# Value chunks in pairs and the output projection in passes of 512 columns

## The chip, the core and the metric

The kernel runs on one core of a Trainium2 chip. The metric is the device time of one execution in microseconds (us). Engines are named as the profile names them: PE (TensorE matmuls), PEld (TensorE weight loads), DVE (VectorE), ACT (ScalarE), POOL (GpSimd), SP (SyncE, which issues the DMAs here).

## The reference

Two layers of a decoder trunk on 256 tokens of width 1024. Each layer normalises x, projects it with one wide matrix, runs four token mixers (block-sparse, three-branch, stick-breaking and dilated attention, called a to d), gates and widens their outputs, merges them with sigmoid gates, and projects the sum back onto x:

```python
def _hybrid_layer(x, norm_w, w_in, cmp_pos, cmp_w1, cmp_w2, w_up, w_out):
    h = _rmsnorm(x, norm_w)
    proj = jnp.einsum('bsd,dc->bsc', h, w_in)          # q, k, v, gates of a..d, merge gates
    ...
    u = jnp.einsum('bsiw,iwd->bsid', widened, w_up)
    y = jnp.sum(merge_g * u, axis=2)
    return x + y @ w_out

def reference(x, ...):
    for layer in range(DEPTH):                          # DEPTH = 2
        x = _hybrid_layer(x, ...)
    return _rmsnorm(x, final_norm_w)
```

The change concerns three products: the values of mixers a and c (columns `av` and `cv` of `w_in`, 256 each) and `y @ w_out` (1024 columns in four blocks of 256, o0 to o3).

## The kernel before

Every product with a weight is made of three products in float32r: the weight is split into a high part (`wh`, an ACT cast) and a low part (`wl`, a DVE subtraction), the activations likewise (`hh` and `hl`), and hi x hi, hi x lo and lo x hi are summed in PSUM. `hh[0]`, `hl[0]` hold the normalised input, `hh[1]`, `hl[1]` hold y, both as 8 slices of the contraction (k = 0 to 7) x 256 tokens.

Weights come as blocks of 128 x 1024 floats ("halves", one DMA each on SP's queue) into 5 `raw` buffers, and from there into 6 buffers each of `wh` and `wl`. `emit_loads`, `run_splits`, `need_splits` and `release` (lines 312 to 376) keep that going; `release` gives a block's buffers back when its last matmul has been emitted.

The program is written out by a planner in Python. `layer_items` (line 36) lists the chunks of a layer: first the pair `('N2', ('av', 'cv'))`, then chunks of queries, keys, gates and values, then 16 pairs of merge (M) and widening (U) chunks, then o0, o1 and the pair o2/o3. `slots_of` (line 1177) turns a chunk into slots, each a generator of matmuls; the main loop (line 1320) runs them and between their steps lets `fill` emit waiting steps of attention and of evacuations. A clock model (`Clock`, `Engine.cost`, line 154) books each instruction, a float32r matmul with 0.000426 us per column, and `pos` holds when each block is due. All engines run their instructions in the order in which they were emitted.

There are two kinds of weight matmul. In T, M and U chunks the weight is stationary and 256 tokens stream. In N chunks (values, o0 to o3) the activations of one 128-token tile are stationary and 256 weight columns stream. The pair av/cv is emitted by `mm_N2` (line 521), which at each step takes the (token tile, chunk, k pair, product) whose operands are ready first and puts the transposes of token tile 1's normalised input (`norm_T`) in between; chunk j accumulates in bank j, both token tiles side by side. `mm_o0` (line 579) does k = 0 to 5 of both token tiles before k = 6, 7, which come last out of the widening stage. o1, o2, o3 use `mm_N`, one slot per token tile and column block.

After a slot of the projection, `out_done` and `post_out` (lines 1123, 1245) add the bank to x (DVE), square it for the norm (ACT) and, in the last layer, multiply with the final norm weight. When a token tile has all four blocks, `norm_a` makes 1/rms and scales the two halves of x; `norm_b` transposes them. For token tile 0 of layer 0 `norm_b` is emitted ahead of the last of the four slots of o2/o3:

```python
if kind == "N2" and name[0] == "o2" and si == 3 and l + 1 < L:
    norm_b(0, pend.pop(0), l + 1)
```

Of the eight PSUM banks three (`pp`) rotate for weight products.

Of the kernel before, what the change touches and what calls it, by code (L numbers as in the profile page):

```python
# [16 lines left out]
L = 2  # L17
# [18 lines left out]
def layer_items():  # L36
# [6 lines left out]
    it += [("N", "o0", 2), ("N", "o1", 2), ("N2", ("o2", "o3"), 4)]  # L43
# [148 lines left out]
def kernel(ctx: ExitStack, tc: tile.TileContext, x_in, w_half, w_kvb, w_up, norm_w, pe_in,  # L192
# [108 lines left out]
    for l, kind, name, n in items:  # L301
        d = {"U": 1.3, "W1": 0.6}.get(kind, 2.6)
        for j in range(n):
            pos.append(p_)
            if not (kind in ("N", "N2", "K") and j % 2 == 0):
                p_ += d if kind not in ("N", "N2", "K") else 2 * d
# [214 lines left out]
    def mm_N2(banks, h0, pend, l):  # L521


        left = {h: 12 for h in range(4)}
        count = [0, 0]
        todo = [(tt, j, kk, p) for tt in range(2) for j in range(2) for kk in range(4) for p in range(3)]
        waits = [(1, j) for j in range(2)]

        def operands(tt, j, kk, p):
            h = h0 + 2 * j + kk // 2  # L530
            if h not in los or (tt, kk // 2) in waits:
                return None
            a = (hh, hh, hl)[p][0][:, 2 * kk:2 * kk + 2, 128 * tt:128 * tt + 128]
            return a, (his, los, his)[p][h]

        n = 0
        while todo:
# [24 lines left out]
            tt, j, kk, p = b  # L562
# [7 lines left out]
            h = 2 * j + kk // 2  # L570
            left[h] -= 1
            if not left[h]:
                release(h0 + h)
            n += 1
            if n % 3 == 0:
                yield
        yield

    def mm_o0(banks, h0):

        for ks in ((0, 1, 2, 3, 4, 5), (6, 7)):
            for tt in range(2):
                for k in ks:
                    hi, lo = (w[h0 + k // 4][:, 256 * (k % 4):256 * (k % 4) + 256] for w in (his, los))
                    a, b = (y[1][:, k, 128 * tt:128 * tt + 128] for y in (hh, hl))
                    o = banks[tt][:, 0:256]
                    mm(o, a, hi, start=(k == 0), stop=False)
                    mm(o, a, lo, start=False, stop=False)
                    mm(o, b, hi, start=False, stop=(k == KT - 1))
                    if k % 2:  # L590
                        yield
# [102 lines left out]
    def post_stack(l, name, bank):  # L694
# [9 lines left out]
        qkv.put(q)  # L704

# [417 lines left out]
    def post_out(l, c, tt, bank):  # L1123
        xs = xt[:, tt, 256 * c:256 * c + 256]
        vec.scalar_tensor_tensor(out=xs, in0=bank[:, 0:256], scalar=0.25, in1=xs, op0=ALU.mult, op1=ALU.add)
        pp.put(bank)
        square(tt, 256 * c, 256 * c + 256, c)
        if l == L - 1:
            if c == 0:
                fin[tt] = [qkv.get(), qkv.get()]  # L1130
            vec.tensor_tensor(out=fin[tt][c // 2][:, 256 * (c % 2):256 * (c % 2) + 256], in0=xs,
                              in1=nws[L][:, 256 * c:256 * c + 256], op=ALU.mult)
# [44 lines left out]
    def slots_of(l, kind, name, h0):  # L1177

        if kind == "N2" and name[0] == "o2":
            for tt in range(2):  # L1180
                for j in range(2):
                    bank = pp.get()
                    yield (lambda: mm_N(bank[:, 0:256], tt, h0 + 2 * j, 256, hh[1], hl[1]),
                           lambda: out_done(l, 2 + j, tt, bank), [h0 + 2 * j, h0 + 2 * j + 1] if tt else [])
        elif kind == "N2":
            banks = [pp.get(), pp.get()]
            yield (lambda: mm_N2(banks, h0, pend.pop(1), l),
# [297 lines left out]
```

## Time and profile before

| | us |
|---|---|
| median of 3 runs (634.63 to 635.20) | 634.83 |
| the profiled execution | 634.86 |
| its span, first to last instruction | 632.9 |
| PE busy | 612.2 (5192 matmuls) |
| DVE busy | 482.1 |
| ACT busy | 369.5 |

The profile is of one execution. Times in its rows are microseconds from the span's start unless marked ns. A matmul's row gives its start and a modelled duration; matmuls are pipelined, so the distance between two starts is what a pass costs when PE is full. `out<-in` names the tile written and the tiles read; "[0.74 <-PE pp]" behind a row says how long the engine was idle before it and on whom it waited.

### The profile page before, as it was taken

What the parts mean: (1) busy time and instruction counts of PE and PEld (TensorE: products, weight loads), DVE (VectorE), ACT (ScalarE), POOL (GpSimd) and SP (SyncE); (2) the same over time, 40 slices, a digit from 0 to 9 for tenths busy, and PEclk for the clock granted to TensorE, in tenths of its full rate; (3) what the DMA queues carried; (4) which work ended last, traced back from release to release, by engine and by line L of the source; (5) the groups of instructions that cost most, each with busy time, mean ns of one, the idle gap of its engine ahead of it and who ended that gap; (6) DMA issues with size and microseconds to landing.
All of it is one profiled execution on the core that took longest, in us unless ns stands there. A gap on an engine that the chain in (4) does not pass through costs nothing.

```text
span 632.9 us, 12881 instructions
## 1 busy us (share of the span) xinstructions
PE 612.2 (97%) x5192; PEld 587.3 (93%) x5192; DVE 482.1 (76%) x850; ACT 369.5 (58%) x657; POOL 46.3 (7%) x59
## 2 busy tenths in 40 slices
PE   7999999999999999999999999999989999999996
PEld 6999999999998999999999899889989989999995
DVE  5887788999976665677688678899999666566673
ACT  5636744655557888445474564543575678864452
POOL 3020100111200000000001101021110000000000
PEclk9999999999999999999999999999999999999998
DMA  8942456644444345677666155645437344466811
GB/s 282 335 147 79 155 192 243 238 162 148 142 161 153 127 140 168 214 246 237 210 211 227 43 192 167 234 168 208 158 100 223 112 166 150 136 205 193 291 62 67
DMA packets 34907, 112.22 MB, mean 177 GB/s; under 512 B 4256, under 2 KB 5280, under 8 KB 34848
## 3 DMA queue, kind: packets, MB, share of 16 engines
q1 hardware_dynamic: 34560, 111.07, 52.2%
q8 instruction: 41, 0.67, 0.4%
q0 software_dynamic: 144, 0.33, 0.3%
q14 instruction: 18, 0.15, 0.1%
q10 hardware_dynamic: 144, 0.00, 0.0%
HBM read 109.61 MB, written 2.10 MB: 177 GB/s over the span
## 4 chain that ended last, share of the span: by engine, by line
PE 64%; DVE 20%; ACT 7%; issue 6%; DMA 2%; POOL 1%; SPq 0%; POOLq 0%; ACTq 0%; DVEq 0%
PE pp L151 55%; DVE wl L151 8%; DVE rope L151 4%; PE psO L151 3%; PE psT L151 3%; ACT p L151 3%; PE psS L151 3%; ACT wh L151 2%; DVE xt L151 2%; DMA raw<-w_half_dram 2%; DVE hl L151 1%; DVE p L151 1%; DVE pd L151 1%; DVE qkv L151 1%; ACT hh L151 1%
## 5 line engine op out<-in xcount | busy, mean ns | idle before, releaser
L151 PE MATMUL pp<-hh,wh 128*128 128x256 f32 x1008 | 288.2, 286 | 2.2 <-DVE xt L151 1.8
L151 PE MATMUL pp<-hh,wl 128*128 128x256 f32 x1008 | 282.1, 280 | 4.5 <-DVE wl L151 4.4
L151 PE MATMUL pp<-hl,wh 128*128 128x256 f32 x1008 | 280.9, 279 | 0.0
L151 DVE TENSOR_TENSOR wl<-raw,wh 128x1024 fp32r<-128x1024 f32 (+2 forms) x198 | 233.1, 1196 | 48.0 <-ACT wh L151 47.2
L151 ACT CAST wh<-raw 128x1024 fp32r<-128x1024 f32 (+2 forms) x198 | 189.2, 979 | 53.7 <-DMA raw<-w_half_dram 24.3
L151 PEld LDWEIGHTS pp<-hh,wh 128*128 128x128 f32 x1008 | 189.4, 188 | 9.0 <-issue 5.5
L151 PEld LDWEIGHTS pp<-hh,wl 128*128 128x128 f32 x1008 | 189.5, 188 | 6.2 <-DVE wl L151 6.1
L151 PEld LDWEIGHTS pp<-hl,wh 128*128 128x128 f32 x1008 | 189.4, 188 | 0.1
L151 PE MATMUL pp<-wh,hh 128*128 128x256 f32 (+1 forms) x320 | 84.9, 285 | 1.0 <-ACT hh L151 1.0
L151 PE MATMUL pp<-wl,hh 128*128 128x256 f32 (+1 forms) x320 | 83.1, 279 | 1.3 <-DVE wl L151 1.2
L151 PE MATMUL pp<-wh,hl 128*128 128x256 f32 (+1 forms) x320 | 83.4, 281 | 0.0
L151 PEld LDWEIGHTS pp<-wh,hh 128*128 128x128 f32 x320 | 58.3, 192 | 2.5 <-ACT hh L151 1.7
L151 PEld LDWEIGHTS pp<-wl,hh 128*128 128x128 f32 x320 | 57.3, 188 | 1.9 <-DVE wl L151 1.9
L151 PEld LDWEIGHTS pp<-wh,hl 128*128 128x128 f32 x320 | 58.0, 191 | 0.0
L151 ACT ACTIVATE p<-p,small 128x128 f32<-128x128 f32 x96 | 40.0, 449 | 27.8 <-DVE small L151 27.1
L151 DVE TENSOR_TENSOR rope<-pp,sinF 32x512 f32<-32x512 f32 x72 | 49.5, 687 | 3.3 <-PE pp L151 1.4
L151 POOL TENSOR_TENSOR xt<-xt,rope 128x512 f32<-128x512 f32 x14 | 28.0, 1998 | 168.8 <-DVE xt L151 93.2
L151 PE MATMUL pp<-widl,wh 128*128 128x256 f32 x128 | 35.9, 281 | 1.1 <-DVE widl L151 1.1
L151 PE MATMUL pp<-widh,wh 128*128 128x256 f32 x128 | 36.0, 282 | 0.0
L151 PE MATMUL pp<-widh,wl 128*128 128x256 f32 x128 | 35.8, 279 | 0.0
L151 ACT ACTIVATE tm<-pp 128x512 f32<-128x512 f32 x32 | 18.9, 591 | 22.1 <-PE pp L151 22.1
L151 ACT COPY ptr<-psT 128x384 f32<-128x384 f32 x47 | 21.4, 478 | 17.6 <-PE psT L151 17.5
(142 smaller groups left out, 666.6 us busy)
## 6 DMA issues: line engine op xcount, KB each, us to landing
raw<-w_half_dram SPq DMA_DIRECT2D x178, 512.0 KB, 4.2
raw<-w_up_dram SPq DMA_DIRECT2D x32, 256.0 KB, 3.2
raw<-w_kvb_dram SPq DMA_DIRECT2D x4, 536.0 KB, 4.5
xt<-x_in_dram SPq DMA_DIRECT2D x4, 256.0 KB, 3.5
xt<-x_in_dram SPq DMA_DIRECT2D x2, 512.0 KB, 7.1
pd<-norm_w_dram SPq DMA_DIRECT2D x2, 512.0 KB, 5.6
x_mem<-xt SPq DMA_DIRECT2D x2, 512.0 KB, 5.4
xt<-x_mem SPq DMA_DIRECT2D x2, 512.0 KB, 6.0
```

The lines of the kernel that those rows point to most:

```text
L151: return f(*a, **k)
```

## The change

The pair av/cv and the two pairs o0/o1 and o2/o3 are done in passes of 512 columns, the widest that one PSUM bank holds. A weight block holds two k slices of all 512 columns of a pair (before: four k slices of 256 columns); the host packs them so (`n2_type`). Each token tile has a bank of its own. o0 and o1 become a pair; its order is k = 0 to 5 of both token tiles, then k = 6, 7 of both. o2/o3 runs token tile 0, then token tile 1; in the last layer token tile 1 is kept in two passes of 256 columns. `post_out` handles n column blocks at once. The values are copied out of PSUM in four pieces of 256 columns, each on the engine (ACT or DVE) that the plan has free first, after the pair's last matmul. The planner's due times and the slot index at which `norm_b` is emitted are adapted (6 of 8 slots instead of 3 of 4).

The diff, cut to its core:

```diff
-    it += [("N", "o0", 2), ("N", "o1", 2), ("N2", ("o2", "o3"), 4)]
+    it += [("N2", ("o0", "o1"), 4), ("N2", ("o2", "o3"), 4)]
...
     def mm_N2(banks, h0, pend, l):
-        left = {h: 12 for h in range(4)}
+        left = [6] * 4
         count = [0, 0]
-        todo = [(tt, j, kk, p) for tt in range(2) for j in range(2) for kk in range(4) for p in range(3)]
+        todo = [(tt, j, p) for tt in range(2) for j in range(4) for p in range(3)]
...
             for i in range(2):
-                k = 2 * kk + i
-                c = count[j]
-                count[j] += 1
-                mm(banks[j][:, 256 * tt:256 * tt + 256], x[0][:, i, :], x[1][:, 256 * (k % 4):256 * (k % 4) + 256],
-                   start=(c == 0), stop=(c == 47))
...
+                c = count[tt]
+                count[tt] += 1
+                mm(banks[tt], x[0][:, i, :], x[1][:, 512 * i:512 * i + 512], start=(c == 0), stop=(c == 23))
...
-            if n % 3 == 0:
+            if n % 2 == 0:
                 yield
...
-    def mm_o0(banks, h0):
...
+    def mm_o(bank, tt, h0, j, c0, c1):
+
+        for i in range(2):
+            k = 2 * j + i
+            hi, lo = (w[h0 + j][:, 512 * i + c0:512 * i + c1] for w in (his, los))
+            a, b = (y[1][:, k, 128 * tt:128 * tt + 128] for y in (hh, hl))
+            o = bank[:, 0:c1 - c0]
+            mm(o, a, hi, start=(k == 0), stop=False)
+            mm(o, a, lo, start=False, stop=False)
+            mm(o, b, hi, start=False, stop=(k == KT - 1))
+            yield
...
+    def post_copy2(l, names, banks):
+
+        for j, name in enumerate(names):
+            T_[l, name] = take(qkv)
+        for tt in range(2):
+            for j, name in enumerate(names):
+                copy_to(T_[l, name][:, 256 * tt:256 * tt + 256], banks[tt][:, 256 * j:256 * j + 256])
+            pp.put(banks[tt])
...
-    def post_out(l, c, tt, bank):
-        xs = xt[:, tt, 256 * c:256 * c + 256]
-        vec.scalar_tensor_tensor(out=xs, in0=bank[:, 0:256], scalar=0.25, in1=xs, op0=ALU.mult, op1=ALU.add)
+    def post_out(l, c, n, tt, bank):
+
+        c0, c1 = 256 * c, 256 * (c + n)
+        xs = xt[:, tt, c0:c1]
+        vec.scalar_tensor_tensor(out=xs, in0=bank[:, 0:c1 - c0], scalar=0.25, in1=xs, op0=ALU.mult, op1=ALU.add)
         pp.put(bank)
-        square(tt, 256 * c, 256 * c + 256, c)
+        square(tt, c0, c1, c)
...
     def slots_of(l, kind, name, h0):
-        if kind == "N2" and name[0] == "o2":
+        if kind == "N2" and name[0] == "o0":
+
+            banks = [pp.get(), pp.get()]
+            for js in ((0, 1, 2), (3,)):
+                for tt in range(2):
+                    for j in js:
+                        yield (lambda: mm_o(banks[tt], tt, h0, j, 0, 512),
+                               (lambda: out_done(l, 0, 2, tt, banks[tt])) if j == 3 else None, [h0 + j] if tt else [], j, tt)
+        elif kind == "N2" and name[0] == "o2":
             for tt in range(2):
-                for j in range(2):
+                last = l == L - 1 and tt
+                for c0, c1 in ((0, 256), (256, 512)) if last else ((0, 512),):
                     bank = pp.get()
...
+                    for j in range(4):
+                        yield (lambda: mm_o(bank, tt, h0, j, c0, c1),
+                               (lambda: out_done(l, 2 + c0 // 256, (c1 - c0) // 256, tt, bank)) if j == 3 else None,
+                               [h0 + j] if tt and c1 == 512 else [], j, tt)
...
-                if kind == "N2" and name[0] == "o2" and si == 3 and l + 1 < L:
+                if kind == "N2" and name[0] == "o2" and si == 6 and l + 1 < L:
                     norm_b(0, pend.pop(0), l + 1)
...
+    def n2_type(w):
+        w = w.reshape(KT, 128, 512).transpose(1, 0, 2)
+        return [w[:, 2 * j:2 * j + 2].reshape(128, -1) for j in range(4)]
```

## Rows read from the trace of the kernel before

**Rows 1.** Page, section 1: busy us, share of the span, instructions.

```profile
PE 612.2 (97%) x5192; PEld 587.3 (93%) x5192; DVE 482.1 (76%) x850; ACT 369.5 (58%) x657; POOL 46.3 (7%) x59
```

**Rows 2.** Stages: stretch, us, busy us by engine (count), PEclk, DMA share, GB/s.

```profile
15.00:24.30 9.30, 9.30 (x84) 9.30 (x83) 7.70 (x9) 6.12 (x7) 0.00 (x0) 1.00 0.96 331
24.30:296.00 271.70, 267.13 (x2286) 256.07 (x2286) 213.17 (x382) 163.53 (x290) 19.62 (x20) 1.00 0.53 177
296.00:330.00 34.00, 33.98 (x296) 33.31 (x295) 23.88 (x33) 17.74 (x33) 1.11 (x2) 1.00 0.65 205
330.00:604.80 274.80, 268.99 (x2298) 257.38 (x2297) 214.53 (x383) 164.03 (x290) 19.48 (x20) 1.00 0.52 175
604.80:626.30 21.50, 21.50 (x192) 21.50 (x191) 13.04 (x23) 7.98 (x20) 0.55 (x1) 1.00 0.11 40
```

**Rows 3.** Timeline of PE, projection of layer 0: start us, us, instruction.

```profile
307.15 0.28 PE L151 MATMUL pp<-wh,hl 128*128 128x256 f32 x1
...
314.97 0.28 PE L151 MATMUL pp<-wh,hl 128*128 128x256 f32 x1
```

**Rows 4.** Timeline of PE, a merge chunk of layer 0.

```profile
177.25 0.28 PE L151 MATMUL pp<-hh,wh 128*128 128x256 f32 x1
...
179.25 0.28 PE L151 MATMUL pp<-hh,wl 128*128 128x256 f32 x1
```

**Rows 5.** Timeline of PE, one score call of branch b in layer 0.

```profile
191.50 0.87 PE L151 MATMUL psS<-hl,hh 128*128 128x256 f32 x4
192.20 0.28 PE L151 MATMUL pp<-hh,wh 128*128 128x256 f32 x1
```

**Rows 6.** Instruction groups by shape: engine, operation, out<-in xcount | busy us, mean ns.

```profile
L151 PE MATMUL psS<-hl,hh 128*128 128x512 f32 x8 | 2.5, 396 | 0.0
L151 DVE SCALAR_TENSOR_TENSOR tm<-tm,pp 128x512 f32<-128x512 f32 x24 | 16.4, 683 | 4.3 <-ACT tm L151 2.4 <-PE pp L151 1.9
L151 DVE SCALAR_TENSOR_TENSOR xt<-pp,xt 128x256 f32<-128x256 f32 x16 | 6.7, 421 | 6.2 <-PE pp L151 6.2
L151 ACT ACTIVATE rope<-xt 128x256 f32<-128x256 f32 x16 | 6.7, 418 | 23.1 <-DVE xt L151 23.1
L151 ACT ACTIVATE rope<-xt 128x512 f32<-128x512 f32 x4 | 2.5, 629 | 2.6 <-DMA xt<-x_in_dram 2.5
```

**Rows 7.** Timeline of PE, bkv chunk of layer 1, next chunk's first

```profile
342.10 0.29 PE L151 MATMUL pp<-wh,hh 128*128 128x268 f32 x1
...
347.92 0.28 PE L151 MATMUL pp<-wh,hl 128*128 128x268 f32 x1
349.12 0.35 PE L151 MATMUL pp<-hh,wh 128*128 128x256 f32 x1 [0.91 <-DVE xt L151]
```

**Rows 8.** Timeline of PE, passes of 32 columns.

```profile
138.31 1.08 PE L151 MATMUL psS<-kct,qkv 128*128 128x32 f32 x8 [0.21 <-DVE kct L151]
```

**Rows 9.** Timeline of PE, the first weight passes of the kernel.

```profile
10.57 0.63 PE L151 MATMUL pp<-wh,hh 128*128 128x256 f32 x2
...
11.21 0.41 PE L151 MATMUL pp<-wh,hl 128*128 128x256 f32 x1
```

**Rows 10.** Timeline of DVE and PE at the layer boundary.

```profile
312.56 0.43 DVE L151 SCALAR_TENSOR_TENSOR xt<-pp,xt 128x256 f32<-128x256 f32 x1 [0.74 <-PE pp L151]
...
314.45 1.42 DVE L151 SCALAR_TENSOR_TENSOR qkv<-xt,rstd,pd 128x512 f32<-128x512 f32 x2 [0.67 <-POOL rstd L151]
...
315.26 1.32 PE L151 MATMUL psT<-iden,qkv 128*128 128x128 f32 x8
...
321.76 1.41 DVE L151 SCALAR_TENSOR_TENSOR qkv<-xt,rstd,pd 128x512 f32<-128x512 f32 x2 [0.66 <-POOL rstd L151]
...
323.47 0.60 PE L151 MATMUL psT<-iden,qkv 128*128 128x128 f32 x4
```

**Rows 11.** Timeline of SP's queue at the end.

```profile
623.62 6.24 SPq L1144 DMA_DIRECT2D out_dram<-qkv  x4
```

**Rows 12.** Timeline of DVE behind the first value pair.

```profile
26.15 3.60 DVE L151 TENSOR_TENSOR wl<-raw,wh 128x1072 fp32r<-128x1072 f32 x3 [1.14 <-ACT wh L151]
```

More of the change, by code (lines that the diff above doesn't have):

```diff
@@ L302 @@
         d = {"U": 1.3, "W1": 0.6}.get(kind, 2.6)
+        if kind == "N2":
+            pos += [p_ + 1.3 * j for j in range(n)]
+            p_ += 4 * d
+            continue
         for j in range(n):
             pos.append(p_)
-            if not (kind in ("N", "N2", "K") and j % 2 == 0):
-                p_ += d if kind not in ("N", "N2", "K") else 2 * d
+            if not (kind in ("N", "K") and j % 2 == 0):
+                p_ += d if kind not in ("N", "K") else 2 * d
     state = dict(at=0, pos=0.0, load=0, hi=0, lo=0)
@@ L704, in post_stack @@
         qkv.put(q)
+    def post_copy2(l, names, banks):
[5 more added lines that the diff above has]
+            pp.put(banks[tt])
+        done.update((l, name) for name in names)
+        return
+        yield
     def post_copy(l, name, bank):
@@ L1243, with out_done @@
     pend = {}
-    def out_done(l, c, tt, bank):
-        post_out(l, c, tt, bank)
-        if c == 3:
+    def out_done(l, c, n, tt, bank):
+        post_out(l, c, n, tt, bank)
+        if c + n == 4:
             if l + 1 < L:
@@ L1294 @@
         weighted(0, 0)
-        square(0, 512, 1024, 1)
+        square(0, 512, 1024, 2)
         norm_rstd(0)
@@ L1298 @@
         square(1, 0, 512, 0)
-        square(1, 512, 1024, 1)
+        square(1, 512, 1024, 2)
         scaled(0, 0, "v")
@@ L1327 @@
             gen = slots_of(l, kind, name, h0)
-            for si, (work, after, freed) in enumerate(gen):
-                if kind == "N2" and name[0] == "o2" and si == 3 and l + 1 < L:
+            for si, (work, after, freed, *part) in enumerate(gen):
+                if kind == "N2" and name[0] == "o2" and si == 6 and l + 1 < L:
                     norm_b(0, pend.pop(0), l + 1)
@@ L1333 @@
                     lo_, hi_ = h0 + si, h0 + si + 1
-                elif kind == "N2" and name[0] == "av":
-                    lo_, hi_ = h0, h0 + 1
                 elif kind == "N2":
-                    lo_, hi_ = h0 + 2 * (si % 2), h0 + 2 * (si % 2) + 2
+                    j, tt = part or (0, 0)
+                    lo_, hi_ = h0 + j, h0 + j + 1
                 else:
@@ L1340 @@
                 state["at"] = lo_
-                first = pos[lo_] + (2.6 if kind in ("N", "K") and si else 0.0)
+                first = pos[lo_] + (2.6 if kind in ("N", "K") and si else 5.2 if kind == "N2" and tt else 0.0)
                 if kind == "W1":
@@ L1349 @@
                     ins = [hl[0]]
-                else:
-                    tt = si // 2 if kind == "N2" else si
-                    ins = [hl[1 if name[0][0] == "o" else 0][:, :, 128 * tt:128 * tt + 128]]
+                elif kind == "N2" and part:
+                    ins = [hl[1][:, 2 * j:2 * j + 2, 128 * tt:128 * tt + 128]]
+                else:
+                    tt = 0 if kind == "N2" else si
+                    ins = [hl[0][:, :, 128 * tt:128 * tt + 128]]
                 run_splits(HORIZON)
@@ L1405, in t_type @@
         return [w[:, :, 128 * j:128 * j + 128].reshape(128, -1) for j in range(w.shape[2] // 128)]
+    def n2_type(w):
+        w = w.reshape(KT, 128, 512).transpose(1, 0, 2)
+        return [w[:, 2 * j:2 * j + 2].reshape(128, -1) for j in range(4)]
     for l in range(L):
         for kind, name, n in layer_items():
-            for nm in (name if kind == "N2" else (name,)):
-                if kind in ("N", "N2") and nm[0] == "o":
-                    c = int(nm[1])
-                    half += n_type(w_out[l][:, 256 * c:256 * c + 256])
-                elif kind in ("N", "N2"):
+            if kind == "N2":
+                if name[0][0] == "o":
+                    c = 256 * int(name[0][1])
+                    half += n2_type(w_out[l][:, c:c + 512])
+                else:
+                    half += n2_type(np.concatenate([w_in[l][:, cols[nm]:cols[nm] + 256] for nm in name], axis=1))
+            for nm in () if kind == "N2" else (name,):
+                if kind == "N":
                     half += n_type(w_in[l][:, cols[nm]:cols[nm] + 256])
```

45 lines of the change are left out of this document (11 added, 34 removed).

## The prediction

> **What bounds the kernel now.** I read the page's first section, then a table of stages, then the PE timeline inside each stage. TensorE (PE) is busy 612.2 of the 632.9 us, and no other engine comes near [rows 1]. The table shows where that is whole: in the three stretches that the change rewrites, the end of the first value pair (15.0 to 24.3), the layer boundary with the output projection and the second value pair (296 to 330) and the last projection (604.8 to 626.3), PE is busy for 9.30 of 9.30, 33.98 of 34.00 and 21.50 of 21.50 us [rows 2]. So there time can come only from what one pass costs, from passes that vanish, or from a new stop. PE's own stops lie in the two long stretches between (267.13 of 271.70 and 268.99 of 274.80 busy) [rows 2], which the diff doesn't touch by name.
>
> A busy engine of pipelined passes is not read by durations (280 ns each, overlapping) but by distances between starts. From 307.15 to 314.97 lie 69 passes of 256 columns: 7.82 / 69 = 0.1133 us each [rows 3]. The same shape runs at a second pace: from 177.25 to 179.25 lie 17, 0.1176 us each [rows 4]. PE's granted clock reads 1.00 in the stages of both [rows 2]. The trace holds long stretches of either pace and changes between them abruptly, so I treat them as two paces, 0.1133 and 0.1178 (the mean over the slow stretches). The three rewritten stretches run at the fast one.
>
> **The change, part by part.** *Passes.* Per layer the value pair has 96 passes of 256 columns, o0 and o1 together 96, o2 and o3 together 96. All become half as many of 512 columns, except the second token tile of o2 and o3 in the last layer, which keeps 48 of 256. That merges 144 pairs in layer 0 and 120 in layer 1, 264 in all; PE goes from 5192 matmuls to 4928. Columns stay the same, so the only question is whether one pass of 512 costs less than two of 256, 2 x 0.1133 = 0.2267.
>
> The trace of before has passes of 512 columns in the same number type: two groups of eight in the scores of branch b [rows 6]. One score call is two passes of 256 and two of 512, and takes 192.20 - 191.50 = 0.70 us; the 256s around run at the slow pace, so a 512 takes (0.70 - 2 x 0.1178) / 2 = 0.232 us [rows 5]. Three other calls that I read so give 0.70 to 0.72. That is 1.97 times the 256 beside it. The cost goes with columns, and little of it is per pass. How to carry this over to stretches at the fast pace is open: scaled by the pace it is 0.232 x 0.1133 / 0.1178 = 0.223, unscaled 0.232. I take the middle, 0.228: 264 x (0.228 - 0.2267) = **+0.3 us**. Ends: below, columns alone at the full level of the clock. The kernel's first passes run at half the pace, three of them from 10.57 to 11.21, 0.2133 each [rows 9], so 512 columns at the full level are 0.2133: 264 x (0.2133 - 0.2267) = -3.5 us. Above, twice the slow pace, 0.2356: +2.4 us.
>
> A rule speaks for a larger gain. The Trainium skill, page "TensorE: Matmul & The Clock Gate", section "Wait — 56ns, not 53.3ns?", gives a warm pass its columns at 2.4 GHz plus a fixed 2.5 ns, 215.7 ns at 512 columns. By it the term would be 264 x (0.2157 - 0.2267) = -2.9 us. The trace's 0.232 for 512 columns [rows 5] and 0.1133 for 256 [rows 3] don't agree with it, so it stays a rival's sentence.
>
> *Layer boundary, token tile 0.* Its last two column blocks were added and squared one after the other; only the second block's add (0.421, DVE) and square (0.418, ACT) stood on the chain to the next layer's normalisation. Now one add of 512 and one square of 512 stand there: 0.683 and 0.629 by the rows of those shapes [rows 6], so +0.26 and +0.21, **+0.47 us**. Does it show? The chain is add at 312.56, scaled halves from 314.45 on DVE, transposes on PE from 315.26 [rows 10]. The pass before the transposes starts at 314.97 [rows 3]; at the pace of 0.1133 the transposes would have come at 315.08, so PE already waits 0.18 us for that chain and nothing hides more. The change puts the transposes after the same share of token tile 1's columns (half), so all of it shows. Bounds 0.3 (one of the two steps partly hidden) and 0.9 (the square queues behind half a cast on ACT).
>
> *Token tile 1.* The same +0.47, hidden: its scaled halves are done at 321.76 + 1.41 = 323.17, the transposes are placed at 323.47 and later [rows 10], and the 48 passes of the next value pair on token tile 0 (48 x 0.1133 = 5.4 us) are there to fill. Uncovered it would be 0.2 us more. 0.
>
> *Copies of the value pair.* Two ACT copies of 512 become four of 256, shared between ACT and DVE by the planner, emitted after the last pass. They wait for the pair's last pass, and behind them on DVE stands a weight subtraction of the next chunk; DVE has 1.14 us of idle time at that place [rows 12], two copies of some 0.35 fit. If that cover goes, the stop of 0.91 us behind DVE [rows 7], where PE waits for a bank that the rotation frees, grows by up to 0.7 in each layer. 0.
>
> *Weight blocks.* Same bytes, same number of loads; a block now holds two of the eight k slices for 512 columns. The first matmuls of a pair need one block instead of two, and the last two y slices are needed after 36 passes of 512 (8 us) instead of 36 of 256 (4 us): looser, but PE doesn't wait there now. Four blocks are held through o0 and o1 instead of two; six buffers leave two for the next pair and blocks come back from the middle on. No load on SP's queue moves past another. 0.
>
> *Start and end.* PE has no idle time in 15 to 24.3 [rows 2], so an earlier operand buys nothing. At the end the last 48 passes and what follows them are as before; token tile 0's output leaves 0.5 later than 623.62, where four issues take 6.24 us in all [rows 11], and the last issues wait for token tile 1 anyway. 0.
>
> **Sum.** 634.86 (the profiled execution; the median of the three runs, 634.83, is the same within 0.03) + 0.3 + 0.47 = 635.6; I say **635.7 us**.
>
> **The rivals.** *Faster: the pass is paced by something fixed.* For it: passes of only 32 columns, eight in 1.08 us with the last one's 0.28 in it, stand (1.08 - 0.28) / 7 = 0.114 apart [rows 8], as far as those of 256. If loading the stationary operand paces both, a 512 is paced by its columns alone: between 0.2133 and 0.2133 + 0.0067 = 0.220 us, a gain of 3.5 to 1.8, middle 2.7: 634.86 - 2.7 + 0.5 = 632.7. Against it: the 512s measured [rows 5], and passes of 268 columns, 47 distances from 342.10 to 347.92, 0.1238 each [rows 7]: 12 columns more cost 0.0105, so columns do set the pace.
>
> *Slower: the 512s run at the slow pace.* Every shape but 256 stands at 0.45 to 0.46 ns per column in this trace (512: 0.232 / 512 = 0.453; 268: 0.462), the slow 256s too (0.460), and only the fast 256s at 0.443 [rows 3, 4, 5, 7]. If 512s know no fast pace, they cost 0.232 to 0.2356, +1.4 to +2.4; and if PE leaves the value pair at the slow pace, the 96 passes behind it in each layer, fast now, lose 96 x 0.0045 = 0.43, twice. 634.86 + 2.0 + 0.5 + 0.5 = 637.9. It decides from a mean distance of 0.230 upwards: there pace and boundary together exceed 1.27 us.
>
> *The planner orders the long stretches anew.* It books 0.218 us for a 512, twice its 0.109, so PE's plan time is unchanged, but the DVE and ACT bookings shift by tenths, and which attention step is filled in where depends on them. What that can be worth: the same work took 271.70 in layer 0 and 274.80 in layer 1 [rows 2], 3.1 apart. Half of that either way, 633 or 637.
>
> **Chances.** Forecast 0.43, faster rival 0.22, slower rival 0.27, planner 0.08, evenly on both sides. A run of this kernel can tell a change from none from about 0.2% on, 1.27 us: faster is under 633.6, slower over 636.1. The forecast's own range (634.4 to 636.6) lies mostly within; a fifth of it lies above. Faster 0.22 + 0.04 = 0.26; slower 0.27 + 0.04 and some 0.05 of the forecast, 0.36; same 0.38. The range takes in the middle of the faster rival and most of the slower one: 632.5 to 638.2.
>
> **What would show it.** In the trace after: 4928 matmuls; distances between the starts of the 512s in the projection of layer 0 (0.228 forecast, under 0.222 for the faster rival, over 0.230 for the slower); the pace of the passes right behind each value pair; the stop ahead of the transposes at the layer boundary, 0.18 now, 0.65 then; both long stretches within 1 us of 271.7 and 274.8. The forecast is wrong if the 512s leave 0.222 to 0.230, if a stop appears in the value pair for a missing block, or if a long stretch moves by more than 1.5 us.

## The result and the profile after

The changed kernel takes **640.17 us** (median of 4 runs, 639.65 to 640.42) where the kernel before takes 635.02 beside it: ratio 1.0081, 95% interval 1.0062 to 1.0099. That is 5.1 us slower, and 2.0 us above the range that was forecast. The profiled execution took 640.39 us with a span of 638.6 (before: 634.86 and 632.9).

The page's first section of the changed kernel: busy us by engine, share of the span, instructions.

```profile
PE 615.2 (96%) x4928; PEld 576.4 (90%) x4928; DVE 482.5 (76%) x843; ACT 367.8 (58%) x644; POOL 46.2 (7%) x59
```

PE has the 264 matmuls less that were counted, and still 3 us more of busy time than in [rows 1]. The table of stages, with the columns of [rows 2], cut at the places in the program that answer to those of before:

```profile
15.00:24.80 9.80, 9.80 (x43) 7.86 (x43) 8.16 (x9) 4.40 (x5) 0.00 (x0) 1.00 0.99 325
24.80:298.70 273.90, 268.41 (x2286) 256.69 (x2286) 214.66 (x385) 163.47 (x290) 19.54 (x20) 1.00 0.51 176
298.70:334.00 35.30, 34.64 (x157) 27.44 (x156) 23.29 (x29) 16.89 (x25) 1.11 (x2) 1.00 0.58 195
334.00:609.50 275.50, 269.76 (x2291) 257.85 (x2290) 214.69 (x383) 164.06 (x292) 19.48 (x20) 1.00 0.51 175
609.50:631.80 22.30, 22.30 (x122) 18.92 (x120) 12.34 (x17) 7.46 (x14) 0.55 (x1) 1.00 0.12 45
```

Every stage is longer. Of the stages that the diff rewrites, the first and the last are still busy from end to end; the middle one has 0.66 us without PE. The longest loss, 2.2 us, is in a stretch that the diff doesn't touch by name. The granted clock is 1.00 in all of them, as before.

The passes of 512 columns in the projection of layer 0, and the transposes of the layer boundary (timeline of PE: start us, us, instruction):

```profile
308.24 0.39 PE L151 MATMUL pp<-wh,hl 128*128 128x512 f32 x1
...
318.04 0.40 PE L151 MATMUL pp<-wh,hl 128*128 128x512 f32 x1
318.85 1.32 PE L151 MATMUL psT<-iden,qkv 128*128 128x128 f32 x8 [0.42 <-DVE qkv L151]
```

Between the first two rows lie 42 distances: 9.80 / 42 = **0.2333 us** for a pass of 512, over the 0.230 from which the slower rival was to decide. Two of 256 at the pace of [rows 3] are 0.2267. After the pass at 318.04 the next could come at 318.27; the transposes come at 318.85, a stop of 0.58 (0.18 before, 0.65 forecast).

Behind the first value pair come 96 passes of T chunks (the weight is stationary and 256 tokens stream; the texts below call them transposed-projection passes). The first and the last of them:

```profile
24.86 0.28 PE L151 MATMUL pp<-hh,wh 128*128 128x256 f32 x1
...
36.05 0.28 PE L151 MATMUL pp<-hh,wl 128*128 128x256 f32 x1
```

(36.05 - 24.86) / 95 = 0.1178: the slow pace, where before they stood at the fast one. The whole difference, from the starts of PE's first pass in each stage in both traces. "Pace" is what the passes of 256 columns and more lie above 0.1133 per 256 columns; bkv is the chunk of 48 passes of 268 columns that follows the 96; the middle of a layer is what lies between bkv and the output projection:

| stage | before us | after us | more | what it is |
|---|---|---|---|---|
| start to first weight pass | 10.20 | 10.63 | +0.43 | the last quarters of x land later in this execution |
| first value pair | 14.15 | 14.23 | +0.08 | pace +0.28, fewer stops at its start |
| 96 passes behind it, bkv chunk | 17.90 | 18.10 | +0.20 | pace +0.42, stop before the next chunk -0.22 |
| middle of layer 0 | 253.78 | 255.71 | **+1.93** | stops behind passes of 256 columns and more +1.85, pace +0.13, distances behind narrower ones -0.05 |
| projection, boundary, second pair | 35.19 | 36.71 | **+1.52** | pace +0.89, stops and transposes +0.64 |
| 96 passes behind it, bkv chunk | 17.90 | 18.12 | +0.22 | pace +0.42, stop -0.20 |
| middle of layer 1 | 255.58 | 256.04 | +0.46 | pace +0.29, stops +0.13 |
| last projection | 21.65 | 22.13 | +0.48 | pace |
| behind the last pass | 6.51 | 6.95 | +0.44 | behind the last output, before the program's end |

The first line is scatter of single executions: over the profiled kernels of this study, which do the same work up to there, the first weight pass starts anywhere from 9.55 to 11.13 us. The last line is not, as the experiments show. What is left to explain is some 5.3 us: passes of 512 and what they leave behind (264 x 0.0066 = 1.74, and 0.84 behind the pairs), the boundary, the middle of layer 0 and the end.

### The profile page after: what moved, and what is told of

It reads as the page before. It is cut to its first block, busy times and chain, and to the rows that moved or that the text cites. A ratio compares the mean times of both kernels' runs of the same rounds, so it can differ in the third digit from the quotient of the medians.

```text
span 638.6 us, 12327 instructions
## 1 busy us (share of the span) xinstructions
PE 615.2 (96%) x4928; PEld 576.4 (90%) x4928; DVE 482.5 (76%) x843; ACT 367.8 (58%) x644; POOL 46.2 (7%) x59
## 4 chain that ended last, share of the span: by engine, by line
PE 61%; DVE 22%; ACT 7%; issue 6%; DMA 1%; POOL 1%; SPq 0%; POOLq 0%; ACTq 0%; DVEq 0%
PE pp L151 53%; DVE wl L151 9%; DVE rope L151 4%; ACT p L151 3%; PE psO L151 3%; PE psT L151 3%; PE psS L151 3%; ACT wh L151 2%; DVE xt L151 2%; DVE p L151 1%; DVE hl L151 1%; DVE pd L151 1%; DVE qkv L151 1%; DMA raw<-w_half_dram 1%; ACT hh L151 1%
## 5 line engine op out<-in xcount | busy, mean ns | idle before, releaser
L151 PE MATMUL pp<-wh,hh 128*128 128x256 f32 (+2 forms) x232 | 73.3, 329 | 1.7 <-ACT hh L151 1.7
L151 PE MATMUL pp<-wl,hh 128*128 128x256 f32 (+2 forms) x232 | 72.6, 326 | 1.5 <-DVE wl L151 1.5
L151 PE MATMUL pp<-wh,hl 128*128 128x256 f32 (+2 forms) x232 | 72.3, 325 | 0.0
L151 PEld LDWEIGHTS pp<-wh,hh 128*128 128x128 f32 x232 | 43.6, 189 | 6.9 <-ACT hh L151 2.3
L151 PEld LDWEIGHTS pp<-wl,hh 128*128 128x128 f32 x232 | 43.5, 188 | 6.3 <-DVE wl L151 2.1
L151 PEld LDWEIGHTS pp<-wh,hl 128*128 128x128 f32 x232 | 43.9, 189 | 4.2 <-DVE hl L151 0.2
```

Of the source, the lines that this page charges most:

```text
L151: return f(*a, **k)
```

## The experiments

Theories at the start: **width** (a pass of 512 costs more than two fast ones of 256, and the passes behind inherit a slow pace), **plan** (the planner orders layer 0's middle anew) and **chain** (the wide add and square at the boundary). The rivals are that the new order of operands, or the four small copies, do it.

**All passes back to 256 columns.** Plan, banks and weight blocks stay.

```diff
-                mm(banks[tt], x[0][:, i, :], x[1][:, 512 * i:512 * i + 512], start=(c == 0), stop=(c == 23))
+                for e in (0, 256):
+                    mm(banks[tt][:, e:e + 256], x[0][:, i, :], x[1][:, 512 * i + e:512 * i + e + 256],
+                       start=(c == 0 and e == 0), stop=(c == 23 and e == 256))
```

(and the same in the output projection)

> The changed kernel with the same plan, banks, weight blocks and order of work; only each pass of 512 columns is issued as two of 256 with the same stationary operand, one behind the other. Theory (width): 512 columns cost 0.2333 us where two of 256 at the fast pace cost 0.2267, and the 96 transposed-projection passes behind each value pair keep the pace that the pair leaves. So 264 x 0.0066 = 1.74 and 2 x 0.43 = 0.85 come back: 640.2 - 2.6 = 637.6 us, with distances of 0.1133 in the rewritten stretches and behind the pairs. Rival (order): the new order of operands and banks brings the slow pace, not the width; then the 256s stand 0.1167 to 0.118 apart and the time stays at 640.2. In both, the long stretch of layer 0 behind 42 us keeps its length, since the plan is the same.

Measured: 639.13 us, before 634.91; 1.0 less than the changed kernel, not 2.6. **Only the pair, the projection left at 512:**

> The changed kernel with only the value pair's passes issued as two of 256 columns; the output projection stays at 512. Width: 2 x 48 merged pairs x 0.0066 = 0.63 come back in the pairs and 0.85 behind them: 640.2 - 1.5 = 638.7 us. If the pace behind the pair has nothing to do with the pair's width: 640.2 - 0.6 = 639.6 us.

Measured: 640.04, a miss by 1.3. The traces say why both fell short. The passes behind the first pair, in the first kernel and in the second, PE timeline:

```profile
25.05 0.28 PE L151 MATMUL pp<-hh,wh 128*128 128x256 f32 x1
...
36.24 0.28 PE L151 MATMUL pp<-hh,wl 128*128 128x256 f32 x1
```

```profile
24.47 0.28 PE L151 MATMUL pp<-hh,wh 128*128 128x256 f32 x1
...
35.24 0.28 PE L151 MATMUL pp<-hh,wl 128*128 128x256 f32 x1
```

The last row of each is a pass of the same place; both lie 95 distances behind the first: 11.19 / 95 = 0.1178 and 10.77 / 95 = 0.1134. Up to there the two programs are the same instruction for instruction. So 256 columns can run at either pace, and which one depends on how PE came into the stretch. The rival of the new order of operands is therefore not excluded for the pairs. In every profiled execution the old pair and the 96 passes behind it stand at 0.1133 (in nine kernels, both layers), and the 96 behind a pair of 512 at 0.1178 (in five kernels, both layers); the new order in passes of 256 gave either: slow in both layers in the first kernel here, fast in both in the second, and slow in layer 0 but fast in layer 1 where the old plan is kept with it (below). The 0.84 behind the pairs came with the passes of 512 each time, but that width alone makes it is not shown. The projections of the first kernel did go back to 0.1133, and its last projection to 21.65 us. In the second kernel both pairs and the passes behind them ran fast, but the middle of layer 0 took 255.94, 0.23 more than in the changed kernel, with some 0.4 more of stops: a part of what PE gained ahead of them was probably taken back by work on other engines that didn't come sooner. Its span is 0.8 shorter; the timed median shows less than that, within the scatter. Neither kernel moved the middle of layer 0 (255.89 and 255.94): the loss there is not made of passes.

**Only the output projection changed**, the value pairs as before:

```diff
-                    half += n2_type(np.concatenate([w_in[l][:, cols[nm]:cols[nm] + 256] for nm in name], axis=1))
+                    for nm in name:
+                        half += n_type(w_in[l][:, cols[nm]:cols[nm] + 256])
```

(with the old pair function, its two copies and its due times)

> Only the output projection is changed; the value pairs are as in the kernel before (passes of 256, a bank per column block, two copies of 512, weight blocks of four k slices). Theory (plan): the plan of layer 0 up to its projection is the kernel before's again, so the stretch from 42 us to the projection loses the 1.9 us that it gained in the changed kernel. 635.0 + 168 x 0.0066 (projection, 1.1) + 0.47 (boundary) + some tenths of plan in layer 1 = 636.6 us, with a first projection pass within 0.3 us of before's 296.0 apart from the start. Rival (no plan effect): the cost in layer 0's middle is from the passes themselves; then it is only the pair's width that goes, 640.2 - 1.5 = 638.7 us.

Measured: 636.7 us (before 634.91), as the plan theory has it. The profiled execution is an odd one at 638.58: ACT waited 4.15 us for a weight block until 24.07, DVE's work behind it came late, and PE stands for 3.3 us at 41 us instead of the 0.9 of before. Behind that stop the granted clock falls to its lower level, 1.2 GHz (0.53 on average from 44.2 to 46.0), and the passes stand 0.21 us apart up to 47.7. The stretch behind the stop is what counts, and it is 253.93 us long with these slow passes in it: before's length, not the changed kernel's.

**The plan alone, from the changed kernel's side.** All passes of 512 stay; two inputs of the planner go back.

```diff
-            pos += [p_ + 1.3 * j for j in range(n)]
+            pos += [p_ + (1.3 * j if name[0][0] == "o" else 2 * d * (j // 2)) for j in range(n)]
...
-                copy_to(T_[l, name][:, 256 * tt:256 * tt + 256], banks[tt][:, 256 * j:256 * j + 256])
+                nc.scalar.copy(T_[l, name][:, 256 * tt:256 * tt + 256], banks[tt][:, 256 * j:256 * j + 256])
```

> The changed kernel with all its passes of 512, banks and weight blocks, but two inputs of the planner as in the kernel before: the value copies are put on ACT by name, and the due times of the value pair's weight blocks are 0, 0, 5.2, 5.2 again instead of 0, 1.3, 2.6, 3.9. The order of DVE's work in layer 0 behind the pair is then the kernel before's. Theory (plan): the 1.9 us that layer 0 lost between 42 us and its projection are the planner's, and come back: 640.2 - 1.9 = 638.3 us, with passes still at 0.2333. Rival (passes): the middle is longer because of the pace that the pair leaves; the plan is worth nothing: 640.2 us.

Measured: 637.45 us, before 635.17. It gives back 2.7 of the 5.1.

**The plan alone, from the other side.** The kernel before, with no pass, copy or block changed; only the due times of the value pair's four weight blocks in each layer.

```diff
-            pos.append(p_)
+            pos.append(p_ + (1.3 * j - (p_ - p0) if kind == "N2" and name[0] == "av" else 0.0))
```

> The kernel before with every pass, copy and weight block as it is; only the due times that the planner holds for the value pair's four weight blocks are those of the changed kernel (0, 1.3, 2.6, 3.9 instead of 0, 0, 5.2, 5.2). DVE then subtracts the pair's third and fourth block two steps earlier, and behind 60 us its order is another, much as in the changed kernel. Theory (plan): the order alone costs what the changed kernel lost in the middle of layer 0 and a little in layer 1: 635.0 + 2.5 = 637.5 us, with more waits of PE for low halves of weights (wl). Rival (the copies): the due times are harmless, the four small copies on DVE are what delays it; then 635.0 us.

Measured: **637.63 us, before 634.96**, ratio 1.0041 (1.0027 to 1.0055). Four due times in the planner's table cost 2.7 us, with the same passes, copies and blocks. What PE waits for in the middle of layer 0 (the rows that differ most among its waits from the first pass behind bkv to the projection: us in total, times, longest), in the kernel before, the changed kernel, the kernel before with new due times, and the changed kernel with the old inputs:

```profile
PE pp L151 <- DVE wl L151: 2.3, 3, 1.3
```

```profile
PE pp L151 <- DVE wl L151: 3.4, 6, 1.6
PE pp L151 <- DVE qkv L151: 0.4, 1, 0.4
```

```profile
PE pp L151 <- DVE wl L151: 3.3, 5, 1.7
PE pp L151 <- DVE qkv L151: 0.4, 1, 0.4
```

```profile
PE pp L151 <- DVE wl L151: 1.9, 3, 1.2
```

With the new due times DVE makes the pair's third and fourth low halves two steps earlier, ahead of the norm's subtractions (`hl`). DVE's timeline there, in the kernel before and in the same kernel with new due times:

```profile
12.79 2.35 DVE L151 TENSOR_TENSOR wl<-raw,wh 128x1024 fp32r<-128x1024 f32 x2
15.05 0.68 DVE L151 TENSOR_TENSOR hl<-psT,hh 128x512 fp32r<-128x512 f32 x1
```

```profile
13.03 4.62 DVE L151 TENSOR_TENSOR wl<-raw,wh 128x1024 fp32r<-128x1024 f32 x4
17.57 1.28 DVE L151 TENSOR_TENSOR hl<-psT,hh 128x512 fp32r<-128x512 f32 x2
```

From 61 us on softmax steps and weight subtractions fall in another order, and PE finds the low half of a weight block (wl) missing five or six times instead of three. The ends of that stretch, for the kernel before with the new due times and for the changed kernel with the old ones (PE timeline, first pass behind bkv and first of the projection):

```profile
43.24 0.36 PE L151 MATMUL pp<-hh,wh 128*128 128x256 f32 x1 [2.20 <-DVE xt L151]
...
298.86 0.28 PE L151 MATMUL pp<-wh,hh 128*128 128x256 f32 x1
```

```profile
43.21 0.36 PE L151 MATMUL pp<-hh,wh 128*128 128x256 f32 x1 [0.68 <-DVE xt L151]
...
296.64 0.39 PE L151 MATMUL pp<-wh,hh 128*128 128x512 f32 x1
```

255.62 and 253.43 us. The last comparison is of **each input alone**. It settles whether the copies count, which the prediction put at nothing: old due times only, old copies only (both in the changed kernel), and new copies only (in the kernel before).

> The changed kernel with the old due times alone (0, 0, 5.2, 5.2); the four value copies stay shared between ACT and DVE. Theory (due times): they alone set layer 0's middle, and the time is that with both old inputs, 637.5 us, middle 253.4. Rival (either input is enough): two of the copies on DVE shift its bookings as well, and DVE's order in this program is still nearly the changed kernel's; then 640.2 us, middle 255.7.

> The changed kernel with the value copies on ACT by name alone; the due times stay 0, 1.3, 2.6, 3.9. Theory (due times): nothing comes back, 640.2 us, middle 255.7. Rival (copies): two small copies on DVE are the cause in this kernel, 637.5 us, middle 253.4.

> The kernel before with its two value copies of 512 as four of 256, shared between ACT and DVE by the planner; the due times are the old ones. DVE's order in the program is unchanged by it. Theory: 635.0 us, middle of layer 0 253.8. Rival (either input is enough): 637.6, middle 255.6.

Measured: 640.76, 639.86 and 635.1 us, before 635.09. In the changed kernel either new input is enough for the new order, so the theory of the due times alone falls; in the kernel before the copies are harmless. Over the kernels of the study the middle of layer 0 comes in two lengths, and with it the time from the last work of DVE or ACT to the end in two values. It goes with the program's order: between 32 us and the projection of layer 0 DVE's instructions come in only two orders in these twelve kernels, one in the five kernels of the shorter middle and the other in the seven of the longer one. Why two copies on DVE bring the new order in the changed kernel and not in the kernel before stays open.

| kernel | due times | copies | middle of layer 0, us | last DVE or ACT work to end, us |
|---|---|---|---|---|
| before | old | old | 253.78 | 3.59 |
| before, new copies | old | new | 253.58 | 3.60 |
| only the projection changed | old | old | 253.93 | 3.59 |
| changed, old planner inputs | old | old | 253.42 | 3.58 |
| the same with 256 columns | old | old | 253.45 | 3.59 |
| before, new due times | new | old | 255.62 | 4.04 |
| changed | new | new | 255.71 | 4.03 |
| changed, old due times | old | new | 255.65 | 4.03 |
| changed, old copies | new | old | 255.55 | 4.04 |
| changed, all 256 | new | new | 255.89 | 4.03 |
| changed, pair 256 | new | new | 255.94 | 4.03 |
| changed, boundary undone | new | new | 255.87 | 4.04 |

So the 0.44 us at the end belong to the plan as well: SP's closing steps behind the last output stand 0.34 us (637.32 to 637.66 in the changed kernel's trace) where they follow at once in the kernel before. Why the program's order shows there is open. 1.9 in the middle and 0.4 at the end are the greater part of the 2.7; the rest is not assigned.

**Plan and width undone together.**

> The old planner inputs (copies on ACT by name, due times 0, 0, 5.2, 5.2) and each pass of 512 as two of 256 with the same stationary operand: of the change only banks, weight blocks, the four copies and the boundary's wide add and square are left. Theory (width and the pace behind it): against the same kernel with 512s, 637.45, the 264 merged pairs give 1.74 and the passes behind the pairs up to 0.85: 634.9 us where the 256s run at 0.1133, and up to 636.3 where a stretch stands at 0.1178 as layer 0's pair did when the 256s were tried under the new plan. Rival (width costs nothing beyond the plan): 637.4 us.

Measured: 635.65 us, before 634.78 (ratio 1.0017, 1.0007 to 1.0026); against the same kernel with 512s 1.8 less, or 1.4 when each is taken against the kernel before that ran beside it (+0.9 and +2.3). Width and what it leaves behind are real. In its trace the first pair and the passes behind it stand at 0.1178, those of layer 1 at 0.1133, which puts it where the expectation had the mixed case (up to 636.3).

**The boundary.** Token tile 0 of o2 and o3 in blocks of 256, each with its own add and square.

```diff
-                last = l == L - 1 and tt
+                last = (l == L - 1) == tt
```

(and the transposes four slots later, which is the same place; in the last layer the square of token tile 0's wide block is made in two halves)

> The changed kernel, but token tile 0 of the last two output column blocks in passes of 256 with a bank, an add and a square for each block, as the last layer's second token tile has it; the norm's transposes stay behind half of token tile 1. Theory (chain): the add and square of 512 instead of 256 on the way to the transposes cost 0.47 us of PE stop; with them undone the stop goes from some 0.65 back to 0.2, and 24 merged pairs less give 0.16: 640.2 - 0.6 = 639.6 us. Rival: the stop stays (the chain waits for something else there): 640.0 us. Its plan behind the boundary may shift by tenths.

Measured: 639.46 us, before 635.17; 0.7 less than the changed kernel, as expected, though the interval of one such comparison (some 0.9 us either way) doesn't carry that alone. The trace does. PE and DVE at its boundary:

```profile
318.24 0.40 PE L151 MATMUL pp<-wh,hl 128*128 128x512 f32 x1
318.57 1.32 PE L151 MATMUL psT<-iden,qkv 128*128 128x128 f32 x8
```

```profile
315.88 0.43 DVE L151 SCALAR_TENSOR_TENSOR xt<-pp,xt 128x256 f32<-128x256 f32 x1 [1.39 <-PE pp L151]
317.77 1.41 DVE L151 SCALAR_TENSOR_TENSOR qkv<-xt,rstd,pd 128x512 f32<-128x512 f32 x2 [0.68 <-POOL rstd L151]
```

And the changed kernel's DVE there:

```profile
315.67 0.69 DVE L151 SCALAR_TENSOR_TENSOR xt<-pp,xt 128x512 f32<-128x512 f32 x1 [1.87 <-PE pp L151]
318.04 1.41 DVE L151 SCALAR_TENSOR_TENSOR qkv<-xt,rstd,pd 128x512 f32<-128x512 f32 x2 [0.67 <-POOL rstd L151]
```

From the add to the scaled halves 1.89 us with 256 columns, 2.37 with 512; PE stands 0.10 us (318.57 - 318.24 - 0.23) and 0.58. The 0.48 us less in the chain and the 0.48 less of stop are the same, so the chain is the whole of it.

**What a pass costs, by width and by history.** Passes appended to the kernel before, behind its last projection; nothing reads their results.

```diff
+        run(48, "T")
+        run(18, "N", 512)
+        run(48, "T")
...
+        for w in (128, 192, 224, 240, 288, 320, 384, 448, 512):
+            run(24, "N", w)
```

> The kernel before with some 1100 passes appended behind its last projection, whose results nothing reads: transposed-projection passes of 256 (stationary weights, moving activations) in groups of 36 to 48, and ahead of the groups 18 passes of 512, of 256 (stationary activations) or of 268 columns, one to three transposes, or one or two passes of 128 columns; then passes of 128 to 512 columns, 24 of each width. It measures the distance of passes by width and what changes the pace. Theory (width sets pace): groups behind 512s and 268s stand 0.1178 apart, those behind 256s of stationary activations 0.1133; 512 costs 0.2333, 320 to 448 some 0.455 ns a column. Rival (phase): the pace of a group depends on how PE came to it and not on the width before it; then groups behind the same width differ, and transposes switch them. If widths under 256 stand 0.1133 apart too, there is a floor there. The time is that of the kernel before plus some 150 us.

PE timeline, three of the groups (24 passes of 384, 24 of 512, and 48 of the transposed kind behind 18 of 512):

```profile
713.59 0.34 PE L151 MATMUL pp<-wh,hh 128*128 128x384 f32 x1
...
717.61 0.34 PE L151 MATMUL pp<-wh,hl 128*128 128x384 f32 x1
...
722.64 0.40 PE L151 MATMUL pp<-wh,hh 128*128 128x512 f32 x1
...
728.01 0.40 PE L151 MATMUL pp<-wh,hl 128*128 128x512 f32 x1
```

```profile
635.40 0.28 PE L151 MATMUL pp<-hh,wh 128*128 128x256 f32 x1
...
640.94 0.28 PE L151 MATMUL pp<-hh,wl 128*128 128x256 f32 x1
```

4.02 / 23 = 0.1748, 5.37 / 23 = 0.2335, 5.54 / 47 = 0.1179. All widths so:

| columns | 128 | 192 | 224 | 240 | 256 | 288 | 320 | 384 | 448 | 512 |
|---|---|---|---|---|---|---|---|---|---|---|
| us apart | 0.1094 | 0.1130 | 0.1124 | 0.1137 | 0.1133 or 0.1178 | 0.1332 | 0.1466 | 0.1746 | 0.2023 | 0.2334 |

Below 256 columns there is a floor of 0.109 to 0.114 us; above, a pass costs 0.452 to 0.463 ns a column at every width tried. At 256 both meet: the fast pace (0.1133) is as far apart as the narrower passes, the slow one (0.1178, 0.460 ns a column) is the price per column. So a pass of 512 had nothing to save: it is two slow 256s (0.2356) less 0.002. The groups behind 512s and 268s stood at 0.1178, as the width theory has it. But of the groups behind three transposes one went to 0.1133 and one not, and 48 passes with stationary activations stayed at 0.1179 once and ran at 0.1133 another time, behind 512s: there the phase rival has the better of it.

Then trials from a slow start: what brings the fast pace back.

> The kernel before with trials appended behind its last projection. Each trial: 4 passes of 268 columns and 12 transposed-projection passes of 256, which the earlier measurement has at 0.118, then one thing that may change the pace (1 to 6 passes of 256 with stationary activations; 3 to 8 transposes; 1 to 6 narrower passes; a stop of PE behind a copy on ACT), then 24 transposed-projection passes whose distance is read; all trials twice. Then one or two passes of 512, 320 or 268 ahead of a group at 0.1133, and other orders of the three products. Theory (address): passes with stationary activations switch to 0.1133 from the second or third on, each time, and the other things don't. Rival (phase): what switches depends on when PE arrives; repeats of a trial differ. The groups behind one 512 stand at 0.118 if a single wide pass is enough to lose the pace.

One pass of 320 or 268 columns, or two of 512, turned a group at 0.1133 into one at 0.1178. Trials repeated with the same passes ahead of them ended the same way both times, which speaks against chance; but passes with stationary activations (1, 2, 3 and 6 of them) never brought the fast pace back here, against the address theory, and two of them lost it. Four passes of 268 left the group behind them fast in some trials and slow in others. **On fixed operands, each trial on two weight buffers:**

> The kernel before with trials appended behind its last projection: four transposes, 18 transposed-projection passes of 256, then one to six passes of another kind, then 30 transposed-projection passes, all on fixed operands, each trial on two weight buffers. The passes behind transposes are expected at 0.118. Theory (phase): the pace is a state that passes of 256 columns keep and that passes of other widths can switch either way; some trial ends at 0.1133, the same on both buffers. Rival: once slow, only passes with stationary activations switch back; then none of the trials with narrower passes ends at 0.1133.

Three kinds ended at 0.1133 on both buffers: three passes of 254, four of 268, one of 260 (two of 128 did on one buffer). The last one (PE timeline):

```profile
799.01 0.28 PE L151 MATMUL pp<-hh,wl 128*128 128x256 f32 x1
799.13 0.28 PE L151 MATMUL pp<-wh,hh 128*128 128x260 f32 x1
799.25 0.28 PE L151 MATMUL pp<-hh,wh 128*128 128x256 f32 x1
...
802.54 0.28 PE L151 MATMUL pp<-hh,wl 128*128 128x256 f32 x1
```

(802.54 - 799.25) / 29 = 0.1134, behind 18 passes at 0.118. If that could be had in the kernel, 300 slow passes at the end of each layer's middle would gain 1.3 us for one pass added.

```diff
+            if l == 0 and t == 0:
+                m(bank[:, 0:260], hh[0][:, 0, 0:128], his[h][:, 0:260], start=True, stop=True)
+            if l != 0 and t == 1:
+                for n, (w, a) in enumerate(((his, hh), (his, hl), (los, hh))):
+                    m(bank[:, 256:510], w[h][:, 0:128], a[0][:, 0, 0:254], start=(n == 0), stop=(n == 2))
```

> The kernel before with four passes more, whose results nothing reads: in layer 0 one of 260 columns with stationary activations ahead of the last branch but one's fourth merge chunk, in layer 1 three transposed-projection passes of 254 columns ahead of the second half of that chunk. From there to the output projection some 300 and 276 passes of 256 follow at 0.1178 without a stop or another width between. Theory (state): the added passes switch PE to 0.1133 as they did in the trials, and it stays so until the projection: -300 x 0.0045 + 0.12 = -1.2 in layer 0 and -276 x 0.0045 + 0.35 = -0.9 in layer 1, 635.0 - 2.1 = 632.9 us. Rival (phase): here they come in at another phase and switch nothing; then their own 0.12 + 0.35 are added, 635.4 us.

Measured: 635.09 us, before 634.9 (ratio 1.0004, 0.9995 to 1.0013). **The two kinds exchanged:**

> As the last one with the two kinds of added passes exchanged between the layers: 254 columns three times in layer 0, 260 once in layer 1. Theory: 632.9 us; if only one kind switches, the trace shows which: 260 alone 635.0 - 1.2 + 0.35 = 634.1, 254 alone 635.0 - 0.9 + 0.12 = 634.2; rival: 635.4 us.

Measured: 635.31, the same ratio. Neither switched anything in either layer:

```profile
261.02 0.28 PE L606 MATMUL pp<-wh,hh 128*128 128x260 f32 x1
261.13 0.28 PE L151 MATMUL pp<-hh,wh 128*128 128x256 f32 x1
...
266.67 0.28 PE L151 MATMUL pp<-hh,wl 128*128 128x256 f32 x1
```

(266.67 - 261.13) / 47 = 0.1179. So the added pass alone doesn't decide. Whether it is the point in PE's rhythm at which the pass falls, as the phase rival has it, or the operands around it, which also differ from the trials', stays open. No version that beats the kernel before came out of this study.

## Why the prediction was wrong

**The sum of the parts**, each by medians: plan 2.7 (new due times alone; 2.7 again when both old inputs are put back), width and the pace it leaves 1.8, boundary 0.55 (0.7 less 0.16 for its 24 merged pairs). Together 5.05 of the 5.15 measured. That it comes so close is in part luck: each part has an interval of 0.6 to 0.9 us either way, the 1.8 is 1.4 against the kernels before that ran beside it, and under the new plan the passes of 256 gave back only 1.0.

Two of the prediction's own signs of being wrong came: the 512s stand at 0.2333, outside 0.222 to 0.230, and the first long stretch went from 271.70 to 273.90, by more than 1.5. Two steps failed: the term of the passes was mis-sized, and the plan, which the sum put at nothing, cost most. The second took the time out of the range: with both old planner inputs, everything else of the change in place, it is 637.45, inside it.

*Passes, forecast +0.3.* The mis-sized term. The 0.232 read from the score calls [rows 5] was right to 0.001 and should have been taken unscaled. The step that failed is the one called open, taking the middle between "scaled by the pace" and "unscaled": passes of 512 were seen at one pace only, and it is 256 that has a cheaper one. 264 x (0.2333 - 0.2267) = +1.74. The rival *slower* had this, with its price and its point of decision, and the inherited pace too (0.42 per layer measured, 0.43 said). The row that spoke for it was in the text: every width but 256 stood at 0.45 to 0.46 ns a column. It should have been the forecast. (Its 637.9 took in 0.5 of the 0.86 that the text gives for the inherited pace; 634.86 + 1.74 + 0.84 + 0.47 is 637.9 again.) The Trainium skill, page "TensorE: Matmul & The Clock Gate", section "Wait — 56ns, not 53.3ns?", with its 215.7 ns for 512 columns, differs from the trace by 18 ns a pass; the trace decides.

*Layer boundary, forecast +0.47.* Right: stop 0.18 to 0.58, and 0.48 between the two ways of doing the add and square.

*The planner, given 8% and half of 3.1 us, on either side; the copies and the blocks, forecast 0.* Wrong: the largest term of the result stood at nothing in the sum. The text argued that PE's plan time was unchanged and that the copies had cover on DVE. But the diff also writes new due times for the pair's blocks, which was not costed at all, and two of the copies now stand on DVE; either is enough in this kernel to reorder layer 0's middle (+1.9, nearly all of it in stops of PE) and to lengthen the end (+0.4). The copies cost nothing as work, as the kernel before with the new copies shows; as an input of the plan they do.

*The rivals as alternatives.* Slower passes, inherited pace and the plan don't exclude each other, and came together. 634.86 + 1.74 + 0.84 + 0.47 + 1.5 = 639.4 could be put together from the text's own terms (1.5 its half of 3.1); the range took in one rival at a time.

*Nothing for token tile 1, weight blocks and start.* Held: apart from the boundary's 0.42, PE has some 0.2 us without work in the stage of projection and pair, and no stop in the first pair from 15 us on. The end was put at 0 for its own work, and that held too; its 0.44 are the plan's. 4928 matmuls as counted.

## What to carry to other kernels

Read the cost of a shape from its distances in the trace at that very shape, and if only one shape stands out as cheaper per column, don't scale others by it. Where a program orders its own work by due times and booked durations, every number that feeds it is part of the change: put the old numbers into the new kernel, or the new ones into the old, one at a time, and time that by itself. Effects that don't exclude each other are added, in the range too.

## What the runs showed of the hardware

In this number type passes stand 0.109 to 0.114 us apart at the widths tried from 128 to 240 columns, and cost 0.45 to 0.46 ns a column above 256, at a granted clock of 1.00. Passes of 256 run at one of two paces, 0.1133 and 0.1178, and stay at it for long stretches (287 passes at 0.1178 from 260.70 to 294.51 in the kernel before). In the trials one wider pass was enough to lose the fast one ahead of T passes, but 48 passes of 256 with stationary activations ran at the fast one behind 24 of 512. The same passes on the same operands ended in the same pace each time; two passes of 128 did so on one weight buffer and not on the other, and the same added pass in another place of the program switched nothing. In the kernel before some 4 of 5 weight passes of 256 in layer 0's middle that follow without a stop run at the slow pace (1326 of 1680), 6.0 us above the fast one. What decides between the paces stays open.
